# Ten of 22 gate and up column tiles of an encoder's feed-forward layers with seven block products in place of eight

## The chip, the cores and the metric

The kernel runs on one core of one Trainium2 chip. The metric is device time in microseconds (us) of one execution, as the median of the runs shown. Each change of layout of the inputs is made on the host before the launch and is not timed. Engines are named as the profile names them: PE is TensorE's matmuls and PEld its weight loads, DVE is VectorE, ACT is ScalarE, POOL is GpSimd, and SP is SyncE, which here only starts DMAs.

## The reference, cut to what is computed

Two layers over 512 tokens of 1024 features. Each layer is a half-step feed-forward block, a mixer with three attention branches, and a second feed-forward block, so there are four feed-forward blocks in all, each with 2816 hidden columns. The change is in these.

```
D_MODEL = 1024; SEQ = 512; DEPTH = 2; D_FF = 2816

def swiglu(h, w_gate, w_up, w_down):
    return (jax.nn.silu(h @ w_gate) * (h @ w_up)) @ w_down

for l in range(DEPTH):
    h = rms_norm(x, norm_g[l, 0])
    x = x + 0.5 * swiglu(h, ffn_w_gate[l, 0], ffn_w_up[l, 0], ffn_w_down[l, 0])
    ...                                    # mixer: x = x + merged @ w_o[l]
    h = rms_norm(x, norm_g[l, 2])
    x = x + 0.5 * swiglu(h, ffn_w_gate[l, 1], ffn_w_up[l, 1], ffn_w_down[l, 1])
return rms_norm(x, final_g)
```

## The kernel before, in words

Activations are held transposed: a tile has 128 features on the partitions and the 512 tokens along the free dimension, so `h` is eight such tiles (`KC` = 8). Each fp32 operand is split into a high part in the type fp32r and a low part, the fp32r of what is left (`hi` and `lo`). A product is then three matmuls for each tile of 128 features: high by high, high by low, low by high. `product` issues them as eight pairs (lines 96 and 97) and then eight more (line 99): 24 matmuls of 512 moving columns.

`ffn` walks over 22 column tiles of 128 hidden columns (`m`). For each it loads the gate's weights and the up weights, 512 KB each. `weights` starts the DMA on SP's queue into a `raw` tile (three buffers), ACT casts the high part (`whi`, line 82), and DVE subtracts to get the low part (`wlo`, line 83); `whi` and `wlo` have four buffers each. PE makes the two products into two PSUM tiles `mm` (three buffers). `gated` scales the gate by the norm's factor `rb` (line 295), ACT applies SiLU (line 296), DVE scales the up product (line 298), multiplies (line 299), and ACT and DVE split the result into `ghi` and `glo` (lines 106 and 108). After the 22 tiles the down product runs over eight output tiles of 66 matmuls each; `advance` adds each to the residual `x`, which lives in DRAM between uses (loaded and kept by DMAs on POOL's queue, `x_tile` and `x_keep`, two buffers of `x`), and makes the next block's `h` from it (`Norm.chunk`). The mixer ends in the same way over eight products with `w_o`. The last block ends in `finish` instead, which has the tokens on the partitions, and transposes `x` beforehand (`x_turned`).

The first block starts with `opening`, which works on the first two column tiles while its inputs are still arriving. The order of instructions on each engine is set when the program is built, by a scheduler with a cost model of its own; on the chip each engine's queue runs in that order, and an instruction that waits holds up all behind it on its engine. PE's sequence is the order of the code.

## Time and profile before

| what | us |
|---|---|
| median of 3 runs | 2484.22 (2482.74 to 2484.49) |
| the profiled execution's own time | 2485.75 |
| its span on the core | 2484.0 |
| PE busy | 2465.3 (99%), 11604 matmuls |
| DVE busy | 1294.3 (52%) |
| ACT busy | 1053.8 (42%) |

The span is what the profile divides up; the time of an execution has a little around it, here 1.75 us. Busy time of PE is modelled and overlapping, so what one matmul costs is read from the distance between starts, not from the durations. Rows of the timeline give the start, the duration, the engine, the line, the operation, and the tiles written and read.

### The profile page before, as it was taken

To read this page: it belongs to the slowest core of one execution; us is meant where nothing else is said; L and a number is where in the kernel's file an instruction comes from. 1 tells how busy PE (TensorE), PEld (TensorE's weight loads), DVE (VectorE), ACT (ScalarE), POOL (GpSimd) and SP (SyncE) were. 2 spreads that over 40 slices of the span, in tenths; PEclk is the share of its full clock that TensorE was granted. 3 is DMA by queue.
4 is the path that set the end of the run, shared out by engine and by line. 5 is a ranking of instruction groups with operands and counts; after the bars stand their busy time and mean duration, and the time that the engine had idled before them with its cause. 6 is when DMAs were issued, how large, how long until landed. Compare 5 with 4: busy or idle time off the path is not lost.

```text
span 2484.0 us, 30196 instructions
## 1 busy us (share of the span) xinstructions
PE 2465.3 (99%) x11604; PEld 2054.7 (83%) x11604; DVE 1294.3 (52%) x2178; ACT 1053.8 (42%) x1776; POOL 193.1 (8%) x300
## 2 busy tenths in 40 slices
PE   8999999999999999999999999999999999999998
PEld 7888888888888888888888888888888888888887
DVE  5444335766666644443344443367676766444432
ACT  5333225755557433332232332267555664333322
POOL 2000003311000000000000000033110001000000
PEclk9999999999999999999999999999999999999999
DMA  5323344432322342233432324443322224332232
GB/s 169 102 94 100 119 131 127 118 103 78 93 85 86 124 128 97 95 98 119 133 107 94 101 91 131 140 118 107 98 86 92 86 83 148 119 115 93 95 100 68
DMA packets 80655, 265.24 MB, mean 107 GB/s; under 512 B 10904, under 2 KB 16328, under 8 KB 80512
## 3 DMA queue, kind: packets, MB, share of 16 engines
q1 hardware_dynamic: 67680, 226.59, 29.4%
q0 software_dynamic: 11680, 34.86, 4.9%
q8 instruction: 92, 1.51, 0.2%
q10 hardware_dynamic: 1152, 1.86, 0.2%
q14 instruction: 51, 0.42, 0.1%
HBM read 241.22 MB, written 12.62 MB: 102 GB/s over the span
## 4 chain that ended last, share of the span: by engine, by line
PE 97%; DVE 1%; ACT 1%; issue 0%; DMA 0%; SPq 0%; POOLq 0%; POOL 0%; ACTq 0%; DVEq 0%
PE mm L96 22%; PE mm L97 22%; PE mm L99 22%; PE mm L288 5%; PE mm L290 5%; PE mm L287 5%; PE av L597 2%; PE t L587 1%; PE s L542 1%; PE s L543 1%; PE av L698 1%; PE mm L492 1%; PE mm L491 1%; PE mm L389 1%; PE mm L387 1%; PE mm L388 1%
## 5 line engine op out<-in xcount | busy, mean ns | idle before, releaser
L96 PE MATMUL mm<-h,whi 128*128 128x512 f32 x2112 | 831.7, 394 | 0.2
L97 PE MATMUL mm<-l,whi 128*128 128x512 f32 x2112 | 825.0, 391 | 0.0
L82 ACT CAST whi<-raw 128x1024 fp32r<-128x1024 f32 (+1 forms) x414 | 429.9, 1039 | 715.3 <-PE mm L97 372.7
L83 DVE TENSOR_TENSOR wlo<-raw,whi 128x1024 fp32r<-128x1024 f32 (+1 forms) x414 | 500.6, 1209 | 294.3 <-ACT whi L82 179.7
L99 PE MATMUL mm<-h,wlo 128*128 128x512 f32 x2112 | 521.8, 390 | 0.0
L99 PEld LDWEIGHTS mm<-h,wlo 128*128 128x128 f32 x2112 | 396.7, 188 | 82.2
L96 PEld LDWEIGHTS mm<-h,whi 128*128 128x128 f32 x2112 | 397.0, 188 | 80.7 <-issue 0.8
L97 PEld LDWEIGHTS mm<-l,whi 128*128 128x128 f32 x2112 | 397.3, 188 | 79.4
L298 DVE TENSOR_TENSOR un<-mm,rb 128x512 f32<-128x512 f32 x87 | 60.1, 691 | 296.8 <-PE mm L99 296.8
L288 PE MATMUL mm<-g,whi 128*128 128x512 f32 x528 | 205.7, 390 | 0.0
L287 PE MATMUL mm<-g,whi 128*128 128x512 f32 x528 | 205.6, 389 | 0.0
L106 ACT CAST g<-un 128x512 fp32r<-128x512 f32 x88 | 54.5, 620 | 251.4 <-DVE un L299 251.4
L290 PE MATMUL mm<-g,wlo 128*128 128x512 f32 x528 | 131.4, 390 | 0.0
L295 DVE TENSOR_TENSOR gn<-mm,rb 128x512 f32<-128x512 f32 x88 | 60.8, 691 | 133.4 <-PE mm L99 133.4
L556 ACT ACTIVATE lg<-lg,negm 128x256 f32<-128x256 f32 (+1 forms) x192 | 114.0, 594 | 25.2 <-DVE negm L553 23.7
L61 POOL DMA_DIRECT2D d_x<-x x40 | 22.1, 553 | 1262.9 <-DVE x L246 1262.6
L288 PEld LDWEIGHTS mm<-g,whi 128*128 128x128 f32 x528 | 99.2, 188 | 20.5
L290 PEld LDWEIGHTS mm<-g,wlo 128*128 128x128 f32 x528 | 99.2, 188 | 20.5
L287 PEld LDWEIGHTS mm<-g,whi 128*128 128x128 f32 x528 | 99.1, 188 | 20.5
L296 ACT ACTIVATE gn<-gn 128x512 f32<-128x512 f32 x88 | 55.8, 634 | 123.6 <-DVE gn L295 123.6
L108 DVE TENSOR_TENSOR g<-un,g 128x512 fp32r<-128x512 f32 x88 | 60.9, 692 | 62.8 <-ACT g L106 62.8
L246 DVE SCALAR_TENSOR_TENSOR x<-mm,x 128x512 f32<-128x512 f32 x40 | 27.7, 692 | 109.1 <-PE mm L290 72.4
(223 smaller groups left out, 3037.8 us busy)
## 6 DMA issues: line engine op xcount, KB each, us to landing
raw<-in_w_gu SPq DMA_DIRECT2D x172, 512.0 KB, 3.4
raw<-in_w_down SPq DMA_DIRECT2D x48, 512.0 KB, 3.5
raw<-in_w_gate SPq DMA_DIRECT2D x48, 512.0 KB, 3.5
raw<-in_w_qk SPq DMA_DIRECT2D x44, 512.0 KB, 3.6
raw<-in_w_branch SPq DMA_DIRECT2D x24, 512.0 KB, 3.5
raw<-in_w_last SPq DMA_DIRECT2D x22, 512.0 KB, 3.5
d_x<-x POOLq DMA_DIRECT2D x40, 256.0 KB, 2.4
x<-d_x POOLq DMA_DIRECT2D x40, 256.0 KB, 2.9
```

Of the source, the lines that this page charges most:

```text
L82: nc.scalar.copy(hi[:, w], raw[:, w])
L83: nc.vector.tensor_tensor(out=lo[:, w], in0=raw[:, w], in1=f(hi[:, w]), op=ALU.subtract)
L96: nc.tensor.matmul(ps, wh, xhi[k], start=k == 0, stop=False)
L97: nc.tensor.matmul(ps, wh, xlo[k], start=False, stop=False)
L99: nc.tensor.matmul(ps, wl, xhi[k], start=False, stop=k == n - 1)
L108: nc.vector.tensor_tensor(out=lo, in0=src, in1=f(hi), op=ALU.subtract)
L287: nc.tensor.matmul(ps, w[k][0], ghi[c + k], start=c + k == 0, stop=False)
L288: nc.tensor.matmul(ps, w[k][0], glo[c + k], start=False, stop=False)
L290: nc.tensor.matmul(ps, w[k][1], ghi[c + k], start=False, stop=c + k == MF - 1)
L295: nc.vector.tensor_tensor(out=gn, in0=pg, in1=h.rb, op=ALU.mult)
L298: nc.vector.tensor_tensor(out=un, in0=pu, in1=h.rb, op=ALU.mult)
L556: nc.scalar.activation(p, p, AF.Exp, bias=negm, scale=-1.0, accum_out=total)
```

## The change

In ten of the 22 column tiles (`SEVEN`; nine in the first block) the work of gate and up is arranged as a product of two matrices of 2 by 2 blocks. The rows of the first are gate and up, its columns the even and the odd tiles of features; the second has the even and the odd tiles of features as rows and the two halves of the tokens (256 each, `H`) as columns. Strassen's scheme in Winograd's form takes seven block products for this where the plain way takes eight. A block product covers four feature tiles and 256 tokens, so it is 12 matmuls of 256 moving columns, and a column tile takes 84 of these in place of 48 of 512.

The scheme needs sums of blocks. Those of the activations (`Sides`, four objects for each block, from the residual `x` times the norm's gain) are made once for each block and held in 16 tiles `side`. Those of the weights (S1 to S4, tiles `wsum`) are made for each of the ten tiles on DVE, and the three weight tiles that come of it are split as before (`parted`), with the eighth block (`w22`) split apart. The scheme's sums of products are made as far as possible in PSUM by accumulating, the rest by ACT copies and DVE additions. The diff, cut:

```diff
+SEVEN = (3, 4, 6, 7, 9, 10, 12, 13, 15, 16)
-    def advance(m, ps, nxt):
+    def advance(m, ps, rb, fp, nxt):
         t = x_tile(m)
-        nc.vector.scalar_tensor_tensor(out=t, in0=ps, scalar=0.5, in1=t, op0=ALU.mult, op1=ALU.add)
+        d = quarters(fp)[:, 0:2, :].rearrange("p a c -> p (a c)")
+        nc.vector.scalar_tensor_tensor(out=d, in0=ps, scalar=0.5, in1=rb, op0=ALU.mult, op1=ALU.mult)
+        nc.vector.tensor_tensor(out=t, in0=d, in1=t, op=ALU.add)
...
     def gated(h, fp, pg, pu, ghi, glo):
...
-        nc.vector.tensor_tensor(out=un, in0=pu, in1=h.rb, op=ALU.mult)
-        nc.vector.tensor_tensor(out=un, in0=un, in1=gn, op=ALU.mult)
+        nc.vector.tensor_tensor(out=un, in0=pu, in1=gn, op=ALU.mult)
...
+    class Sides:
+        def __init__(self, fp, h, p, xs):
...
+                    x = x_tile(k)
+                nc.scalar.activation(x, x, AF.Copy, scale=h.gain[:, k : k + 1])
...
+            nc.vector.tensor_tensor(out=t1, in0=b12, in1=b11, op=ALU.subtract)
+            nc.vector.tensor_tensor(out=t2, in0=b22, in1=t1, op=ALU.subtract)
+            nc.vector.tensor_tensor(out=t3, in0=b22, in1=b12, op=ALU.subtract)
+            nc.vector.tensor_tensor(out=t4, in0=b21, in1=t2, op=ALU.subtract)
+            both = [split(raw[:, n : n + 2, :].rearrange("p a c -> p (a c)"), fp, "side", 16) for n in (0, 2)]
...
+    def seven(l, i, m, h, fp, sides, ghi, glo):
...
+        ra, a11, a12 = raw(0)
+        wa = parted(ra)
+        rb, a21, a22 = raw(1)
+        w22 = [fp.tile([P, 4, P], F32R, tag=g, name=g) for g in ("w22h", "w22l")]
+        nc.scalar.copy(w22[0], a22)
+        nc.vector.tensor_tensor(out=w22[1], in0=a22, in1=f(w22[0]), op=ALU.subtract)
...
+        nc.vector.tensor_tensor(out=s1, in0=a21, in1=a22, op=ALU.add)
+        nc.vector.tensor_tensor(out=s3, in0=a11, in1=a21, op=ALU.subtract)
+        w13 = parted(r1)
+        nc.vector.tensor_tensor(out=s2, in0=s1, in1=a11, op=ALU.subtract)
+        nc.vector.tensor_tensor(out=s4, in0=a12, in1=s2, op=ALU.subtract)
+        w24 = parted(r2)
...
+        block_product(pa[:, 0], blocks(wa, 0, 2 * P), [s.b11 for s in sides], start=True)
+        block_product(pr[:, 0], blocks(w13, 0), side(1), start=True)
+        nc.scalar.copy(u2, pa[:, 0])
+        block_product(pv[:, 0], [[t[:, k, :] for k in range(4)] for t in w22], side(4), start=True, stop=True)
+        nc.scalar.copy(pv[:, 1], pr[:, 0])
+        block_product(pa[:, 0], blocks(wa, P, 2 * P), [s.b21 for s in sides])
+        block_product(pa[:, 1], blocks(w24, 0), side(2), stop=True)
+        nc.vector.tensor_tensor(out=u2, in0=pa[:, 1], in1=u2, op=ALU.add)
+        nc.scalar.copy(c11, pa[:, 0])
+        block_product(pr[:, 0], blocks(w24, S), [s.b22 for s in sides])
+        block_product(pr[:, 1], blocks(w13, S), side(3), stop=True)
+        nc.vector.tensor_tensor(out=gu[:, 1:3], in0=pr, in1=u2.unsqueeze(1).to_broadcast([P, 2, H]), op=ALU.add)
+        nc.vector.tensor_tensor(out=c21, in0=pv, in1=u3.unsqueeze(1).to_broadcast([P, 2, H]), op=ALU.add)
+        nc.vector.tensor_tensor(out=gn, in0=gn, in1=h.rb, op=ALU.mult)
+        nc.scalar.activation(gn, gn, AF.Silu)
         nc.vector.tensor_tensor(out=un, in0=un, in1=gn, op=ALU.mult)
+        keep(fp, un, ghi, glo)
```

The fourth block product accumulates onto the first one's result, so PE waits before it until ACT has copied that result to `u2`. In every ordinary tile one DVE multiplication by `rb` goes; `advance` has one more DVE instruction in its place, and `finish` takes the factor from a small tile. `Sides` is emitted after the second tile (after the third in the first block, where it reads the inputs already on chip). In `finish`'s block the transposes of `x` move from tiles 4 to 11 to tiles 17 to 20, two in each, with four small ACT copies for each in place of one. Tiles `g` of the late columns, `x` of the opening and other small buffers share space with the new tiles. The three buffers of `raw`, four of `whi` and `wlo`, two of `x` and three of `mm` stay as they were.

How the queues change is shown at three places. The numbers in the names tell one use of a tile from another; what stands in brackets is what the instruction waits for (DMAHW and DMASW are landings of DMAs).

On DVE, in the middle of the first block, one ordinary column tile before:

```order
L295 TENSOR_TENSOR gn_1063<-mm_1013,rb_357 128x512 [waits PE_49]
L83 TENSOR_TENSOR wlo_1147<-raw_1145,whi_1146 128x1024 [waits DMAHW3_49,Activation_49]
L298 TENSOR_TENSOR un_1066<-mm_1038,rb_357 128x512 [waits PE_49]
L83 TENSOR_TENSOR wlo_1153<-raw_1151,whi_1152 128x1024 [waits DMAHW4_49,Activation_49]
L299 TENSOR_TENSOR un_1066<-un_1066,gn_1063 128x512 [waits DVE_49]
L108 TENSOR_TENSOR g_1071<-un_1066,g_1069 128x512 [waits Activation_49]
```

On DVE now, while PE is in ordinary tile 11 (`gu_1458` is its work): the end of tile 10 (`gu_1298`), the sums for tile 12 (`raw_1466`, `wsum_1485`) and those for tile 13 (`raw_1593`, `raw_1599`, `wsum_1605`, `wsum_1612`):

```order
L389 TENSOR_TENSOR wsum_1485<-wsum_1478,raw_1466 128x512
L390 TENSOR_TENSOR wsum_1485<-raw_1466,wsum_1485 128x512 [waits DVE_49]
L431 TENSOR_TENSOR gu_1298<-gu_1298 128x512 [waits Activation_49]
L385 TENSOR_TENSOR wsum_1605<-raw_1599 128x512 [waits DMAHW6_49]
L332 TENSOR_TENSOR gu_1458<-mm_1408,rb_357 128x512 [waits PE_49]
L120 TENSOR_TENSOR g_1394<-gu_1298,g_1392 128x512 [waits Activation_49]
L95 TENSOR_TENSOR wlo_1489<-wsum_1485,whi_1488 128x1024
L386 TENSOR_TENSOR wsum_1605<-raw_1593,raw_1599 128x512 [waits DMAHW5_49]
L389 TENSOR_TENSOR wsum_1612<-wsum_1605,raw_1593 128x512 [waits DVE_49]
L390 TENSOR_TENSOR wsum_1612<-raw_1593,wsum_1612 128x512 [waits DVE_49]
L334 TENSOR_TENSOR gu_1458<-mm_1433,gu_1458 128x512 [waits PE_49,Activation_49]
L95 TENSOR_TENSOR wlo_1596<-raw_1593,whi_1595 128x1024 [waits Activation_49]
```

A landing of a DMA now stands between DVE's sums: `raw_1599` is the third `raw` buffer over again, the one that held `raw_1466`, whose last reader is the L390 two rows above it.

On ACT at that place before, one tile:

```order
L82 CAST whi_1080<-raw_1079 128x1024 [waits DMAHW2_49,PE_49,Activation_49]
L106 CAST g_997<-un_994 128x512 [waits DVE_49]
L82 CAST whi_1146<-raw_1145 128x1024 [waits DMAHW3_49,PE_49,Activation_49]
L296 ACTIVATE gn_1063<-gn_1063 128x512 [waits DVE_49,Activation_49]
L82 CAST whi_1152<-raw_1151 128x1024 [waits DMAHW4_49,PE_49,Activation_49]
```

and now, from the cast of S2 and S4 for tile 12 to the copy of tile 12's first block product (`u2`, L415):

```order
L94 CAST whi_1488<-wsum_1485 128x1024 [waits DVE_49,PE_49]
L118 CAST g_1392<-gu_1298 128x512 [waits DVE_49]
L333 ACTIVATE gu_1458<-gu_1458 128x512 [waits DVE_49]
L86 CAST whi_1595<-raw_1593 128x1024 [waits DMAHW5_49,PE_49]
L118 CAST g_1462<-gu_1458 128x512 [waits DVE_49]
L415 COPY gu_1495<-mm_1492 128x256 [waits PE_49,Activation_49]
```

The copy for which PE waits stands behind the cast of tile 11's result (`g_1462`), which waits for DVE's L334 above.

At the end of a down product, DVE before (`x_2628` is the last of the eight residual tiles, `l7_2635` its low part for the next product):

```order
L83 TENSOR_TENSOR wlo_2758<-raw_2756,whi_2757 128x1024 [waits DMAHW1_49,PE_49,Activation_49]
L246 SCALAR_TENSOR_TENSOR x_2628<-mm_2561,x_2628 128x512 [waits DMASW7_49,DMASW0_49,PE_49]
L83 TENSOR_TENSOR wlo_2788<-raw_2786,whi_2787 128x1024 [waits DMAHW2_49,Activation_49]
L127 SCALAR_TENSOR_TENSOR l7_2635<-x_2628,ng_75,h7_2633 128x512 [waits Activation_49]
L137 TENSOR_TENSOR acc_1959<-acc_1959,sq_2637 128x512 [waits Activation_49]
```

and now:

```order
L259 SCALAR_TENSOR_TENSOR gu_3173<-mm_3104,rb_357 128x512 [waits PE_49]
L87 TENSOR_TENSOR wlo_3333<-raw_3331,whi_3332 128x1024 [waits DMAHW2_49,Activation_49]
L260 TENSOR_TENSOR x_3171<-gu_3173,x_3171 128x512 [waits DMASW7_49,DMASW0_49,DVE_49]
L139 SCALAR_TENSOR_TENSOR l7_3180<-x_3171,ng_75,h7_3178 128x512 [waits Activation_49]
L149 TENSOR_TENSOR acc_2490<-acc_2490,sq_3182 128x512 [waits Activation_49]
```

The residual is now made in two instructions with a weight's low part between them.

At the end of the mixer, ACT before (`h7` is the last tile of the next block's input):

```order
L125 ACTIVATE h6_7548<-x_7543,ng_75 128x512 [waits DVE_49]
L136 ACTIVATE sq_7552<-x_7543 128x512 [waits Activation_49]
L82 CAST whi_7697<-raw_7696 128x1024 [waits DMAHW0_49,PE_49]
L125 ACTIVATE h7_7591<-x_7586,ng_75 128x512 [waits DVE_49]
L136 ACTIVATE sq_7595<-x_7586 128x512 [waits Activation_49]
```

and now:

```order
L137 ACTIVATE h6_8093<-x_8088,ng_75 128x512 [waits DVE_49]
L148 ACTIVATE sq_8097<-x_8088 128x512 [waits Activation_49]
L86 CAST whi_8240<-raw_8239 128x1024 [waits DMAHW0_49,PE_49]
L348 ACTIVATE x_8303<-x_8303,ng_75 128x512 [waits DMASW5_49,DMASW1_49,DMASW6_49,DVE_49,Activation_49]
L137 ACTIVATE h7_8136<-x_8131,ng_75 128x512 [waits DVE_49]
L148 ACTIVATE sq_8140<-x_8131 128x512
```

The first `x` of `Sides` has come in ahead of `h7`, and waits for its DMA.

More of the change, by code (lines that the diff above doesn't have):

```diff
@@ L83, in weights, with parted @@
             nc.vector.tensor_tensor(out=lo[:, w], in0=raw[:, w], in1=f(hi[:, w]), op=ALU.subtract)
+        return hi, lo
+    def parted(src, dst=None):
+        hi = wpool.tile([P, 1024], F32R, tag="whi", name="whi")
+        lo = wpool.tile([P, 1024], F32R, tag="wlo", name="wlo")
+        nc.scalar.copy(hi, src)
+        nc.vector.tensor_tensor(out=lo, in0=src, in1=f(hi), op=ALU.subtract)
         return hi, lo
@@ L253, in ffn @@
             first = l == 0 and i == 0
+            xs = [None] * KC
             xt = None
             if first:
-                opening(l, i, h, fp, ghi, glo)
+                xs = opening(l, i, h, fp, ghi, glo)
+            sides = []
             for m in range(2 if first else 0, MF):
+                if m in (SEVEN[1:] if first else SEVEN):
+                    if not sides:
+                        sides = [Sides(fp, h, p, xs) for p in range(4)]
+                    seven(l, i, m, h, fp, sides, ghi, glo)
+                    continue
                 wg = weights(a["w_gu"][l, i, m, 0])
@@ L267, in ffn @@
                     h.finish()
-                if m == 4 and first:
+                if m == 5 and first:
                     position_tables()
                     small_values()
-                if nxt is None and 4 <= m < 4 + KC:
-                    if m == 4:
-                        xt = fp.tile([P, 4, D], F32, tag="xt", name="xt")
-                    x_turned(xt, m - 4)
+                if nxt is None and MF - 5 <= m < MF - 1:
+                    if xt is None:
+                        xt = x_room(fp)
+                    for k in range(2):
+                        x_turned(xt, 2 * (m - MF + 5) + k)
                 gated(h, fp, pg, pu, ghi, glo)
+                if m == (2 if first else 1):
+                    sides = [Sides(fp, h, p, xs) for p in range(4)]
             if nxt is None:
-                finish(fp, ghi, glo, xt)
+                finish(fp, ghi, glo, xt, h)
                 return
@@ L290, in ffn, with quarters, keep @@
                         nc.tensor.matmul(ps, w[k][1], ghi[c + k], start=False, stop=c + k == MF - 1)
-                advance(m, ps, nxt)
+                advance(m, ps, h.rb, fp, nxt)
+    def quarters(fp):
+        return fp.tile([P, 5, H], F32, tag="gu", name="gu", bufs=2)
+    def keep(fp, un, ghi, glo):
+        late = len(ghi) > SEVEN[-1]
+        hi, lo = split(un, fp, "side" if late else "g", 16 if late else GBUFS)
+        ghi.append(hi)
+        glo.append(lo)
     def gated(h, fp, pg, pu, ghi, glo):
-        gn = fp.tile([P, S], F32, tag="gn", name="gn", bufs=2)
+        t = quarters(fp).rearrange("p a c -> p (a c)")
+        gn, un = t[:, 0:S], t[:, S : 2 * S]
@@ L299, in gated @@
         nc.vector.tensor_tensor(out=un, in0=un, in1=gn, op=ALU.mult)
-        hi, lo = split(un, fp, "g", 2 * MF)
-        ghi.append(hi)
-        glo.append(lo)
+        keep(fp, un, ghi, glo)
     def opening(l, i, h, fp, ghi, glo):
@@ L312, in opening @@
         raws = [wpool.tile([P, 1024], F32, tag="raw", name="raw", bufs=3) for _ in range(3)]
-        raws.append(fp.tile([P, 1024], F32, tag="raw4", name="raw4"))
+        raws.append(fp.tile([P, 1024], F32, tag="sum", name="raw4", bufs=2))
         def load(k, queue):
-            xs[k] = fp.tile([P, S], F32, tag=f"xf{k}", name="xf")
+            xs[k] = fp.tile([P, S], F32, tag="g", name="xf", bufs=GBUFS)
             queue.dma_start(xs[k], a["xT"][k])
@@ L358, in opening, with x_room @@
         gated(h, fp, ps[2], ps[3], ghi, glo)
+        return xs
+    def x_room(fp):
+        side = [fp.tile([P, S], F32, tag="side", name="xt", bufs=16) for _ in range(6)]
+        t = fp.tile([P, 2, S], F32, tag="sum", name="xt", bufs=2)
+        side += [t[:, 0], t[:, 1]]
+        return [side[2 * t : 2 * t + 2] for t in range(4)]
     def x_turned(xt, k):
@@ L365, in x_turned, with finish @@
             nc.tensor.transpose(pt[:, j, :], t[:, j * P : (j + 1) * P], ident)
-        nc.scalar.copy(xt[:, :, k * P : (k + 1) * P], pt)
-    def finish(fp, ghi, glo, xt):
+        for j in range(4):
+            nc.scalar.copy(xt[j][k // 4][:, k % 4 * P : (k % 4 + 1) * P], pt[:, j])
+    def finish(fp, ghi, glo, xt, h):
         half = D // 2
-        fg = fp.tile([P, D], F32, tag="fg", name="fg")
+        fg = fp.tile([P, D], F32, tag="sum", name="fg", bufs=2)
         nc.scalar.dma_start(fg, a["final_g"].to_broadcast([P, D]))
@@ L421, in finish @@
             nc.gpsimd.tensor_tensor(out=r, in0=r, in1=nhalf[:, 0:1], op=ALU.pow)
[L422 removed]
+            x0 = xt[t][0]
             nc.scalar.activation(x0, x0, AF.Copy, scale=r)
```

55 lines of the change are left out of this document (50 added, 5 removed).

## The prediction

> **What bounds the kernel now.** I read first the page: the busy row of the engines, the clock by slices, and the chain that ended last.
>
> ```profile
> PE 2465.3 (99%) x11604; PEld 2054.7 (83%) x11604; DVE 1294.3 (52%) x2178; ACT 1053.8 (42%) x1776; POOL 193.1 (8%) x300
> PEclk9999999999999999999999999999999999999999
> PE 97%; DVE 1%; ACT 1%; issue 0%; DMA 0%; SPq 0%; POOLq 0%; POOL 0%; ACTq 0%; DVEq 0%
> ```
>
> PE is the bound from end to end at a full clock, so PE time saved counts, as long as DVE (52%) and ACT (42%) still deliver in time. Then I read PE's timeline, in an ordinary column tile and where the mixer has matmuls of 256 columns.
>
> ```profile
> 150.73 0.39 PE L96 MATMUL mm<-h,whi 128*128 128x512 f32 x1
> 154.36 1.98 PE L99 MATMUL mm<-h,wlo 128*128 128x512 f32 x8
> 156.17 0.39 PE L96 MATMUL mm<-h,whi 128*128 128x512 f32 x1
> 161.61 0.39 PE L96 MATMUL mm<-h,whi 128*128 128x512 f32 x1
> ...
> 493.82 0.28 PE L491 MATMUL mm<-whi,h 128*128 128x256 f32 x1
> 495.74 1.13 PE L494 MATMUL mm<-wlo,h 128*128 128x256 f32 x8
> 496.71 0.28 PE L542 MATMUL s<-qk 128*128 128x256 f32 x1
> ```
>
> A tile of 48 matmuls takes 161.61 - 150.73 = 10.88 us, 226.7 ns each. Sixteen matmuls of 256 columns, each with new weights, take 495.74 - 493.82 = 1.92 us, 120.0 ns each. Half the columns cost 53%.
>
> **PE's gain.** A changed tile is 84 x 0.120 = 10.08 us, 0.80 less. In 9 + 3 x 10 = 39 tiles that is 31.2 us (1.26%). The transposes only move, at the same count.
>
> Here a rule can be weighed. The Trainium skill's TensorE: Matmul & The Clock Gate (Back-to-back issue gap) gives 518 cycles for 512 columns and 262 for 256 at 2.4 GHz, 215.8 and 109.2 ns; by it, as an estimate, a tile would gain 1.19 us and the sum 46 us. The rows above disagree by about 11 ns on either, and the measurement decides.
>
> **DVE and ACT in the changed tiles.** These rows price their work and the handing over between engines.
>
> ```profile
> 150.93 0.69 DVE L295 TENSOR_TENSOR gn<-mm,rb 128x512 f32<-128x512 f32 x1 [1.64 <-PE mm L99]
> 156.37 0.69 DVE L298 TENSOR_TENSOR un<-mm,rb 128x512 f32<-128x512 f32 x1 [3.62 <-PE mm L99]
> 156.98 1.22 DVE L83 TENSOR_TENSOR wlo<-raw,whi 128x1024 fp32r<-128x1024 f32 x1
> 158.11 0.69 DVE L299 TENSOR_TENSOR un<-un,gn 128x512 f32<-128x512 f32 x1
> 159.48 0.69 DVE L108 TENSOR_TENSOR g<-un,g 128x512 fp32r<-128x512 f32 x1 [0.69 <-ACT g L106]
> ...
> 151.72 0.63 ACT L296 ACTIVATE gn<-gn 128x512 f32<-128x512 f32 x1 [1.50 <-DVE gn L295]
> 154.60 1.05 ACT L82 CAST whi<-raw 128x1024 fp32r<-128x1024 f32 x1 [2.25 <-PE mm L97]
> 158.83 0.62 ACT L106 CAST g<-un 128x512 fp32r<-128x512 f32 x1 [3.18 <-DVE un L299]
> ...
> L590 DVE TENSOR_TENSOR pl<-t,ph 128x256 fp32r<-128x256 f32 x64 | 26.8, 419 | 3.3 <-ACT ph L589 2.9
> L589 ACT CAST ph<-t 128x256 fp32r<-128x256 f32 x64 | 23.5, 367 | 25.2 <-PE t L587 24.7
> L125 ACT ACTIVATE h<-x,ng 128x512 fp32r<-128x512 f32 x40 | 29.0, 724 | 47.2 <-DVE x L246 47.2
> ...
> raw<-in_w_gu SPq DMA_DIRECT2D x172, 512.0 KB, 3.4
> x<-d_x POOLq DMA_DIRECT2D x40, 256.0 KB, 2.9
> ```
>
> From start to start DVE takes 0.61 us for 512 elements (156.37 to 156.98) and 1.13 for 1024 (156.98 to 158.11); a dependent one follows at its full 0.69; 256 take about 0.34 (0.42 less the same overlap). DVE to ACT is 0.10 (150.93 + 0.69 to 151.72), ACT to DVE 0.03 (158.83 + 0.62 to 159.48), ACT after PE's last use of a buffer 0.24 (154.36 to 154.60).
>
> A changed tile needs on DVE three splits of 1024, ten instructions of 512 (w22, S1 to S4, two sums of products, `rb`, the product, `glo`) and one of 256: 3 x 1.13 + 10 x 0.61 + 0.34 = 9.8 us of PE's 10.08; an ordinary one 2 x 1.13 + 3 x 0.61 = 4.1. Two changed and one ordinary are 23.7 us of DVE in 31.04 of PE (10.08 x 2 + 10.88). The total fits; what decides is the order. I follow one round by hand, pair 9 and 10, ordinary 11, then 12, with zero at tile 9's start on PE and 1.44 us for a block product.
>
> - At 9.60 PE has read the high part of tile 9's seventh product's weights; ACT may cast S2, S4 of tile 10 into that buffer: 9.84 to 10.89.
> - DVE from 10.92: that low part 1.13, tile 9's sum 0.61, a low part of 11 at 1.13, the second sum 0.61, `rb` 0.69: 15.09.
> - SiLU (0.10 + 0.63 + 0.03), product 0.69, cast (0.10 + 0.62 + 0.03): 17.29. DVE had nothing else there.
> - DVE then, in its order: `glo` 9, S1 of 12, low part of 11, `u2` of 10, `w22` of 12, S3 of 12, low part, sum of 10, low part, second sum, `rb`, S2, S4: eight of 0.61, three of 1.13, one of 0.34 and S4 at a full 0.69 with 0.08 for its dependence, 9.4: 26.7. The SiLU and casts for these run beside.
> - Only now is the `raw` buffer of tile 12's first weights free for tile 13's second, and S1 of 13 stands next but one on DVE. The DMA takes 3.4 and 0.08 at its ends: 30.15. DVE stands still for some 3 us.
> - DVE: S1 of 13, `gn` 11, `glo` 10, low part of 12, S3, S2, S4 (0.08 more), product of 11: 5.5, 35.7.
> - ACT casts tile 11's result (0.10 + 0.62), then copies tile 12's `u2` (0.37, 0.10 of it overlapped); with 0.07 to PE the fourth block product may start at 36.8.
>
> PE wants it at 31.04 + 3 x 1.44 = 35.36. So PE waits 1.4 us, and with a slow first matmul after it 1.5, in each round; the next round starts later by as much, so it is not made up. A round costs 32.5 us against 32.64 before: the gain of two tiles, 1.6, is nearly all given back. This wait comes at tiles 6, 9, 12 and 15 of three blocks and at 9, 12, 15 of the first (there tile 4 stands alone, and the same sum leaves tile 6 half a us to spare): 15 x 1.5 = 22.5 us.
>
> **The first pair in blocks two to four.** `Sides` goes through two `x` buffers in four rounds: each is a load (0.4 to issue, 2.9), two ACT scales at 0.63 and four DVE instructions of 0.34, 6 us at least, with waits for casts and ordinary work in the same queues. The second `x` comes when the last residual is stored.
>
> ```profile
> 881.25 0.55 POOL L56 DMA_DIRECT2D x<-d_x  x1 [2.62 <-DMA d_x<-x]
> 886.53 0.55 POOL L56 DMA_DIRECT2D x<-d_x  x1 [2.46 <-DMA d_x<-x]
> 882.23 0.39 PE L96 MATMUL mm<-h,whi 128*128 128x512 f32 x1
> 883.15 0.72 ACT L125 ACTIVATE h<-x,ng 128x512 fp32r<-128x512 f32 x1 [1.48 <-DVE x L246]
> 885.63 0.39 PE L97 MATMUL mm<-l,whi 128*128 128x512 f32 x1
> ...
> 373.97 0.69 DVE L246 SCALAR_TENSOR_TENSOR x<-mm,x 128x512 f32<-128x512 f32 x1 [2.80 <-PE mm L290]
> 374.58 1.22 DVE L83 TENSOR_TENSOR wlo<-raw,whi 128x1024 fp32r<-128x1024 f32 x1
> 375.71 0.75 DVE L127 SCALAR_TENSOR_TENSOR l<-x,ng,h 128x512 fp32r<-128x512 f32 x1
> 377.17 0.39 PE L97 MATMUL mm<-l,whi 128*128 128x512 f32 x1
> ...
> 33.45 0.69 DVE L295 TENSOR_TENSOR gn<-mm,rb 128x512 f32<-128x512 f32 x1
> 34.38 0.39 PE L96 MATMUL mm<-h,whi 128*128 128x512 f32 x1
> ```
>
> From 4.3 us into the block (886.53 - 882.23) four such rounds of 6 to 6.5 end at 28 to 30, and what stands behind on DVE (three `side` and `gn` instructions, a low part, S2, S4: 4.4) puts tile 3's S4 near 33.9. Then the same DMA wait (3.5), three sums and a low part of DVE, a cast and the copy (4.1): 41.5. Tile 3 starts near 34.8 and wants its fourth product at 39.1: 2.4 us. Nothing and 4 us bound it; three blocks, 7 us.
>
> **At the seams.** After a down product the residual's second instruction comes behind the low part, at 375.71; then `h7` to 377.22 and `l7` to 378.0, with 0.07 to PE, which wants it at 377.17: 0.9 us, three times. After the mixer the first `x` lands at 881.25 + 2.9 = 884.15, its scale precedes `h7` (before at 883.15) and moves it to 884.83 to 885.55, `l7` to 886.3 against 885.63: 0.8, twice. Together 4.3; bounds 0 (if the scheduled waits fall elsewhere) and 7. In the opening the sums of `Sides` (about six DVE instructions before `gn`, now at 33.45) move `gn` past 34.38, when PE wants the bank: 1.0, between 0 and 3. SP has no more DMAs, POOL eight more loads in each of three blocks, of which only those above are waited for. The late transposes' `x` loads (2.9) have a tile of 10.88 us to land, and the small ACT copies lie beside PE. The instruction saved in ordinary tiles is off the path: nothing.
>
> **The sum.** -31.2 + 22.5 + 7 + 4.3 + 1.0 = +3.6 us on the profiled execution (span 2484.0, time 2485.75, 1.5 above the median). On the median of 2484.2 that is 2488. A measurement tells about 0.2%, 5 us, from no change.
>
> **Rivals.**
> 1. DVE is early enough, so the landing is hidden: no waits in the pairs, and 2484.2 - 31.2 + 5.3 = 2458. For it: 7 us of DVE are free in a round. Against it: buffer and order tie S1 to S4 by the DMA, and DVE would have to be 1.4 us earlier. 17%.
> 2. Half of that: a round is 1 us shorter, from overlaps that I take too small. 2484.2 - 31.2 + 15 x 0.5 + 3 x 1.3 + 5.3 = 2470. 12%.
> 3. DVE's new shapes (sums over strided blocks, a broadcast operand) run longer than the 0.69 of plain ones. Ten of them stand in a round's chain, so 0.1 us on each is 1 us, 15 us in all: 2503. It decides for slower from 0.01 us on each (1.5 us above the forecast). No row shows such a shape slower, or at all. 13%.
> 4. The matmuls of a changed tile don't keep 120 ns; 1 ns is 3.3 us. The 256-column rows are the same operation, with weights new in each, so I fold this into the range.
>
> The forecast has 58%, with a range of its own of 2480 to 2496; it splits into faster 6, same 28, slower 24. With the rivals: faster 0.35, same 0.28, slower 0.37. The range over all reaches into the first and third: 2460 to 2503.
>
> **What would show it.** After: 13008 matmuls, 256-column ones 0.120 apart. In tiles 9 to 11 PE's waits at the fourth block product, about 1.5 us, released by ACT's `u2` copy; DVE idle near 3 us before S1 of each pair's second tile, released by a landing; a round of 32.5 us. I am wrong if these waits are absent (rival 1), or if the round is over 33 with DVE instructions longer than 0.7.

## The result, and the profile after

The changed kernel takes 2461.78 us (median of 4 runs, 2460.08 to 2466.55) against 2483.94 before: the ratio is 0.9916, with an interval of 0.9903 to 0.9928. That is 22 us faster, where the prediction had 2488 and gave faster a chance of 0.35. The time is within 4 us of the first rival's, 2458. A second set of runs of the same kernel gave 2461.56 (2458.19 to 2468.34).

The page of the changed kernel, its busy row, the clock by slices, and the chain by engine:

```profile
PE 2437.5 (99%) x13008; PEld 2094.9 (85%) x13008; DVE 1517.9 (62%) x2562; ACT 1184.3 (48%) x2057; POOL 207.7 (8%) x324
PEclk9999999999999999999999999999999999999999
PE 95%; DVE 1%; issue 1%; DMA 1%; ACT 1%; POOL 0%; POOLq 0%; ACTq 0%; DVEq 0%
```

PE is still the bound. The span went from 2484.0 to 2459.3 us, 24.7 less, and all of it lies on PE's own line: from its first matmul to its last are 2470.9 us before and 2446.1 after. So 6.5 of the 31.2 us were given back, not 34.8 as forecast.

The round that the prediction worked out by hand (pair 9 and 10, tile 11, then 12 and 13) starts here at 110.17. PE's timeline of tile 12, its first, fourth and next tile's first block product:

```profile
141.23 0.28 PE L400 MATMUL mm<-h,whi 128*128 128x256 f32 x1
...
145.54 0.28 PE L400 MATMUL mm<-h,whi 128*128 128x256 f32 x1
...
151.30 0.28 PE L400 MATMUL mm<-h,whi 128*128 128x256 f32 x1
```

The tile takes 151.30 - 141.23 = 10.07 us, 119.9 ns for each of 84 matmuls. The round takes 141.23 - 110.17 = 31.06, where 31.04 was the ideal and 32.5 the forecast. The fourth block product comes 4.31 us after the first, without a wait. DVE's timeline around the landing for which it was to stand still:

```profile
129.24 0.69 DVE L386 TENSOR_TENSOR wsum<-raw 128x512 f32<-128x512 f32 x1
...
133.91 0.68 DVE L389 TENSOR_TENSOR wsum<-wsum,raw 128x512 f32<-128x512 f32 x1
134.63 0.69 DVE L390 TENSOR_TENSOR wsum<-raw,wsum 128x512 f32<-128x512 f32 x1
135.24 0.69 DVE L431 TENSOR_TENSOR gu<-gu 128x512 f32<-128x512 f32 x1
135.84 0.68 DVE L385 TENSOR_TENSOR wsum<-raw 128x512 f32<-128x512 f32 x1
...
141.50 0.69 DVE L334 TENSOR_TENSOR gu<-mm,gu 128x512 f32<-128x512 f32 x1 [0.70 <-PE mm L111]
```

L386 is S3 of tile 12, L390 its S4, L385 S1 of tile 13. S1 follows with no idle time. At the end DVE waits 0.70 us for PE's tile 11, not the other way round. SP's queue in the same stretch shows why:

```profile
129.99 0.33 SPq L370 DMA_DIRECT2D raw<-in_w_gu  x1
135.39 0.33 SPq L85 DMA_DIRECT2D raw<-in_w_gu  x1
```

And ACT's timeline shows how much time is left before PE needs the copy:

```profile
142.22 0.62 ACT L118 CAST g<-gu 128x512 fp32r<-128x512 f32 x1 [1.55 <-DVE gu L334]
142.92 0.38 ACT L415 COPY gu<-mm 128x256 f32<-128x256 f32 x1
```

The load for tile 13's second weights is issued at 129.99, right behind the end of S3 (129.93), and not behind S4 (135.32). S3 is the last reader of the *second* weights of tile 12. The addresses in the built program agree: the tile `raw_1599` lies at 71584 like `raw_1472`, the second weights of tile 12; `raw_1466`, the first, lies at 75680 and goes to tile 14. The `u2` copy ends at 143.30, 2.24 us before PE wants its fourth product.

By stretch, from the starts of the down products on PE (254.09, 1123.02 and 1483.49 before, 246.87, 1109.76 and 1462.64 after; each down stage takes 119.68 in both): counted from PE's first matmul, the first block gained 7.3 us of its 7.2 (9 tiles by 0.80), the first mixer with block 2 gained 6.0 of 8.0, block 3 7.6 of 8.0, and all that follows 3.9 of 8.0. Most of what was given back is at the ends of the mixers, 1.2 and 4.0 us. The second mixer's end on ACT:

```profile
2094.78 0.72 ACT L348 ACTIVATE x<-x,ng 128x512 f32<-128x512 f32 x1 [4.19 <-DMA x<-d_x]
2095.40 0.71 ACT L137 ACTIVATE h<-x,ng 128x512 fp32r<-128x512 f32 x1
```

On PE:

```profile
2096.16 0.49 PE L108 MATMUL mm<-h,whi 128*128 128x512 f32 x1 [1.68 <-ACT h L137]
2096.95 0.79 PE L109 MATMUL mm<-l,whi 128*128 128x512 f32 x1 [0.29 <-DVE l L139]
2097.54 3.21 PE L111 MATMUL mm<-h,wlo 128*128 128x512 f32 x8
```

And a window over these slow matmuls (length, then busy time and instructions of PE, PEld, DVE, ACT and POOL, the granted clock, and DMA):

```profile
2098.00:2100.20 2.20, 2.20 (x7) 1.71 (x6) 0.00 (x0) 0.82 (x1) 0.07 (x1) 0.52 0.45 119
```

`Sides`' scale of x (L348) stands ahead of `h7` (L137) on ACT and waits for its load, as the prediction said. PE loses 2.4 us by waiting, measured by the starts. Then come some eight matmuls at a granted clock of 0.52 and 427 ns, 1.6 us more. The first mixer's end costs 1.2 us at 879.33 and 880.12. In the profiles of other kernels below, the two places cost 1 to 11 us together, by run.

In the opening, DVE's timeline:

```profile
29.08 0.42 DVE L354 TENSOR_TENSOR tsum<-xf,tsum 128x256 f32<-128x256 f32 x1
29.41 0.42 DVE L355 TENSOR_TENSOR tsum<-xf 128x256 f32<-128x256 f32 x1
29.75 0.15 DVE L169 TENSOR_SCALAR rt<-st 128x4 f32<-128x4 f32 x1
29.82 1.22 DVE L87 TENSOR_TENSOR wlo<-raw,whi 128x1024 fp32r<-128x1024 f32 x1
30.95 0.42 DVE L356 TENSOR_TENSOR tsum<-xf,tsum 128x256 f32<-128x256 f32 x1
31.29 0.68 DVE L120 TENSOR_TENSOR side<-tsum,side 128x512 fp32r<-128x512 f32 x1
```

POOL's, after:

```profile
29.99 1.95 POOL L170 TENSOR_TENSOR rs<-rt,nhalf 128x4 f32<-128x4 f32 x1 [11.01 <-DVE rt L169]
```

POOL's, before:

```profile
30.94 1.04 POOL L158 TENSOR_TENSOR rs<-rt,nhalf 128x4 f32<-128x4 f32 x1 [11.82 <-DVE rt L157]
```

PE's, after:

```profile
32.00 0.65 PE L176 MATMUL st<-ident,rs 128*128 128x128 f32 x4 [2.19 <-POOL rs L170]
```

`rt`, from which POOL takes the power for the norm's factor, stands behind two sums of `Sides` on DVE. The power then takes 1.95 us in place of 1.04, beside a DVE subtraction that ends at 31.04; in the kernel before, no DVE instruction ran beside it. PE's start at 32.00 is 2.35 us later than its pace without a wait would give. In this one profile the first inputs came sooner than in that of before (waits of 1.0 at 6.77 and 0.4 us at 8.88 against 3.4 at 9.10), 2.0 us in sum, so the first block as a whole kept its full gain by luck. Why they came sooner, no run here settles.

### The profile page after: what moved, and what is told of

It reads as the page before. It is cut to its first block, busy times and chain, and to the rows that moved or that the text cites. A ratio compares the mean times of both kernels' runs of the same rounds, so it can differ in the third digit from the quotient of the medians.

```text
span 2459.3 us, 33723 instructions
## 1 busy us (share of the span) xinstructions
PE 2437.5 (99%) x13008; PEld 2094.9 (85%) x13008; DVE 1517.9 (62%) x2562; ACT 1184.3 (48%) x2057; POOL 207.7 (8%) x324
## 3 DMA queue, kind: packets, MB, share of 16 engines
q8 instruction: 102, 1.67, 0.3%
## 4 chain that ended last, share of the span: by engine, by line
PE 95%; DVE 1%; issue 1%; DMA 1%; ACT 1%; POOL 0%; POOLq 0%; ACTq 0%; DVEq 0%
PE mm L111 16%; PE mm L108 16%; PE mm L109 16%; PE mm L313 5%; PE mm L312 5%; PE mm L315 5%; PE mm L400 2%; PE pr L403 2%; PE pr L401 2%; PE pr L400 2%; PE mm L403 2%; PE mm L401 2%; PE av L738 2%; PE t L728 1%; PE s L683 1%
## 5 line engine op out<-in xcount | busy, mean ns | idle before, releaser
L86 ACT CAST whi<-raw 128x1024 fp32r<-128x1024 f32 (+1 forms) x336 | 347.7, 1036 | 509.1 <-PE mm L109 196.2
L108 PE MATMUL mm<-h,whi 128*128 128x512 f32 x1488 | 587.7, 395 | 2.4 <-ACT h L137 2.2
L109 PE MATMUL mm<-l,whi 128*128 128x512 f32 x1488 | 582.2, 391 | 0.6 <-DVE l L139 0.6
L87 DVE TENSOR_TENSOR wlo<-raw,whi 128x1024 fp32r<-128x1024 f32 (+1 forms) x336 | 405.5, 1207 | 256.6 <-ACT whi L86 145.8
L111 PE MATMUL mm<-h,wlo 128*128 128x512 f32 x1488 | 368.9, 390 | 0.0
L111 PEld LDWEIGHTS mm<-h,wlo 128*128 128x128 f32 x1488 | 280.3, 188 | 58.5
L108 PEld LDWEIGHTS mm<-h,whi 128*128 128x128 f32 x1488 | 279.7, 188 | 59.0 <-ACT h L137 3.9
L109 PEld LDWEIGHTS mm<-l,whi 128*128 128x128 f32 x1488 | 279.9, 188 | 56.7 <-DVE l L139 2.0
L312 PE MATMUL mm<-g,whi 128*128 128x512 f32 x408 | 158.7, 389 | 0.0
L313 PE MATMUL mm<-g,whi 128*128 128x512 f32 x408 | 158.7, 389 | 0.0
L95 DVE TENSOR_TENSOR wlo<-wsum,whi 128x1024 fp32r<-128x1024 f32 x78 | 95.2, 1220 | 44.5 <-ACT whi L94 44.5
L334 DVE TENSOR_TENSOR gu<-mm,gu 128x512 f32<-128x512 f32 x48 | 33.1, 689 | 86.1 <-PE mm L111 86.1
```

Source lines behind the costliest of these rows:

```text
L86: nc.scalar.copy(hi[:, w], raw[:, w])
L87: nc.vector.tensor_tensor(out=lo[:, w], in0=raw[:, w], in1=f(hi[:, w]), op=ALU.subtract)
L108: nc.tensor.matmul(ps, wh, xhi[k], start=k == 0, stop=False)
L109: nc.tensor.matmul(ps, wh, xlo[k], start=False, stop=False)
L111: nc.tensor.matmul(ps, wl, xhi[k], start=False, stop=k == n - 1)
L312: nc.tensor.matmul(ps, w[k][0], ghi[c + k], start=c + k == 0, stop=False)
```

## The experiments

The theory after the result (A): buffers are given out as they fall free and not in turn, so no landing stands in DVE's way, and DVE has room. The rival (B): buffers don't matter and DVE was only overpriced. Ratios are against the kernel before, with their intervals.

**The three `raw` buffers strictly in turn.**

```diff
+    def raw_tile():
+        n = turn_raw[0] % 3
+        turn_raw[0] += 1
+        return wpool.tile([P, 1024], F32, tag=f"raw{n}", name="raw", bufs=1)
```

> The three raw buffers are three tiles used strictly in turn. Theory A (what my forecast got wrong is the rule by which buffers are given out: not in turn but in the order in which they come free): with them in turn the second load of a pair's second tile must follow S4 of the first tile, 5 us later than in the changed kernel (there it was issued at 129.99, S3 ended at 129.93, S4 at 135.33). The scheduler has put three DVE instructions more ahead of S1 of the second tile, which take up 1.8 us of it, so DVE should stand 0.5 to 1 us for the landing. PE's fourth block product waited for nothing and had 2.2 us to spare after the u2 copy (112.23 against 114.49), so the time stays at 2462, at most 2466. The forecast's own chain would still give 1.5 us in each of 15 rounds: 2484. Theory B (buffers don't matter, DVE was simply overpriced): load issued right after S3 or DVE without any wait for a landing, 2462.

Measured: 2463.68 us (2458.22 to 2472.22), 0.9921 [0.9906, 0.9936]. SP at the same place:

```profile
134.69 0.33 SPq L377 DMA_DIRECT2D raw<-in_w_gu  x1
```

DVE there:

```profile
133.94 0.69 DVE L397 TENSOR_TENSOR wsum<-raw,wsum 128x512 f32<-128x512 f32 x1
...
137.04 0.68 DVE L127 TENSOR_TENSOR g<-gu,g 128x512 fp32r<-128x512 f32 x1
138.10 0.69 DVE L392 TENSOR_TENSOR wsum<-raw 128x512 f32<-128x512 f32 x1 [0.38 <-DMA raw<-in_w_gu]
```

The load now follows S4 (ended 134.63), and DVE stands for the landing, but 0.38 us and not 3: the scheduler, which knows of the buffer, has put other work first (tile 10's product, tile 11's gate, the low part of S2 and S4, and tile 10's `glo`). PE does not wait. So the mechanism exists, and buffers do matter to the loads. The forecast had joined a real order of instructions to an assumed use of buffers, and these two belong to different programs.

**`whi` and `wlo` in turn as well.**

```diff
+        return wpool.tile([P, 1024], F32R, tag=f"{g}{n}", name=g, bufs=1)
```

> As the one before, and the four whi and wlo buffers are used strictly in turn too. Theory A: the cast of S2 and S4 of a pair's second tile then starts when PE has read the seventh product's high part, at 9.84 us of the tile before as I had worked out by hand, not at 8.42 as in the changed kernel. With 1.4 us later here and 0.5 to 1 us of DVE standing for the landing, the 2.2 us to spare are used up to 0 or a little below: rounds of 31.1 to 31.6 us, 2462 to 2470. My forecast's full chain: rounds of 32.5, 2484. Theory B: no change at all, 2462, and rounds of 31.06.

Measured: 2463.29 us (2461.58 to 2469.74), 0.9922 [0.9910, 0.9933]; pairs start every 31.06 us, and the `u2` copy keeps its 2.25 us before nearly every fourth product. All the buffers that the forecast assumed in turn are in turn here, and the wait is not there. The cast of S2 and S4 of tile 10 did begin 9.80 us into the round, as the forecast's 9.84 had it, but the scheduler had moved the sums of tile 12 forward, and its S4 ended at 19.9 in place of the forecast's 26.7. So the expected loss of slack did not come either. In time and pace (B) foretold this run better than (A); what speaks against (B) is the run before it, where the load moved behind S4 with its buffer. Both have it that DVE has room, and that is what keeps the time. No run joins the forecast's order of instructions to buffers in turn, so the forecast's wait in the rounds was never produced.

**How late may DVE be?** S2 is computed three times in each changed tile (the diff), or five times.

```diff
-        nc.vector.tensor_tensor(out=s2, in0=s1, in1=a11, op=ALU.subtract)
+        for _ in range(3):
+            nc.vector.tensor_tensor(out=s2, in0=s1, in1=a11, op=ALU.subtract)
```

> In each changed tile S2 is computed three times in place of once: two more DVE instructions of 512 (1.2 us by their distance) in the chain of sums, 2.4 us in a round of two changed tiles and an ordinary one, in which DVE is busy 73.59 of 93.20 us, so 6.5 of 31.06 free. Theory (order and buffers leave DVE room, PE's fourth product has 2.25 us to spare): no wait, 2460 to 2466. The forecast's chain, in which DVE's time in a round counts in full: 13 rounds or so and six pairs by 2.4 us, 2490 to 2500.

> S2 computed five times: four more, 2.4 us in each changed tile, 4.9 in a round of 6.5 free. Theory: two changed tiles beside each other then need 2 x (9.8 + 2.4) = 24.4 us of DVE in 20.2 of PE, made up in the ordinary tile; the low parts of S2 and S4 come late by up to 2 us, and PE begins to wait, 0 to 2 us a round: 2462 to 2490. Forecast's chain: 2520 and more.

Measured: 2459.53 us (2458.96 to 2462.16), 0.9906 [0.9892, 0.9919], and 2465.82 (2463.40 to 2469.67), 0.9931 [0.9918, 0.9945]. Windows over three rounds of the first block (the columns as above), of the changed kernel:

```profile
78.00:172.00 94.00, 94.00 (x650) 87.50 (x649) 74.79 (x111) 47.83 (x70) 3.21 (x6) 1.00 0.32 107
```

With two more:

```profile
78.00:172.00 94.00, 94.00 (x652) 87.83 (x651) 81.25 (x122) 47.93 (x70) 3.22 (x6) 1.00 0.32 107
```

With four more:

```profile
78.00:172.00 94.00, 94.00 (x650) 87.28 (x649) 88.90 (x134) 45.48 (x69) 3.22 (x6) 1.00 0.32 104
```

DVE goes from 74.79 to 81.25 and 88.90 us of 94, and PE loses nothing in this stretch. In the third kernel the copy's lead before the fourth product falls to 0.05 to 2.25 us, and PE begins to wait here and there (0.9 us at 1271), 2.3 us in all by the starts of the tiles. So 2.4 us more of DVE in a round are free. Twice that is 4 us slower in the median, which the overlapping intervals do not set apart from nothing; the profile shows 2.3 of it as waits. The forecast's chain had charged every such microsecond to PE.

**More tiles with seven products.** Tiles 3, 4 and 6 to 16; then all of 3 to 16.

```diff
+SEVEN = (3, 4, 6, 7, 8, 9, 10, 11, 12, 13, 14, 15, 16)
```

> Seven products in tiles 3, 4 and all of 6 to 16 of each block (without 3 in the first): three tiles more in each of four blocks, 12 x 0.80 = 9.6 us less of PE. A changed tile needs 9.8 us of DVE by my count of 0.61 and 1.13 us starts, PE 10.08. Theory A (buffers come as they fall free, DVE's queue keeps ahead): PE doesn't wait in the run of eleven, tiles 10.08 apart: 2452. Theory of the forecast (DVE's queue meets landings and is late): with no ordinary tile to recover in, DVE falls behind by 0.5 to 1.5 us in each tile of the run, tiles 10.6 to 11.6 apart, 44 tiles: 2475 to 2520.

Measured: 2451.48 us (2450.62 to 2453.16), 0.9872 [0.9859, 0.9885]: the fastest of all, 10 us below the changed kernel for 12 tiles more. A window in the run of eleven:

```profile
101.00:181.00 80.00, 80.00 (x669) 80.00 (x668) 77.49 (x111) 44.47 (x72) 0.00 (x0) 1.00 0.31 100
```

DVE is busy 97% and PE doesn't wait; tiles start 10.08 apart. A changed tile's 9.8 us of DVE, as the prediction counted them, fit into 10.08. Outside that window PE waits once for `u2`, 1.4 us in the first pair of block 3.

> Seven products in all of tiles 3 to 16 (in the first block without 3 and 5): 12 + 3 x 14 = 54 tiles in place of 39 (51 in the run with 13). Theory: DVE keeps up with 9.8 us in 10.08 (it did in the run of eleven, busy 97%), so 3 x 0.80 = 2.4 less than 2451.5: 2449. Rival: the first pair has no ordinary tile behind it in which DVE makes up for Sides, and PE waits 1 to 5 us in tiles 4 to 8 of three blocks: 2452 to 2464.

Measured: 2456.02 us (2454.56 to 2456.70), 0.9889 [0.9875, 0.9902]: more tiles and 4.5 us slower. A window in the third block:

```profile
1299.00:1400.00 101.00, 98.33 (x814) 97.66 (x813) 94.79 (x135) 55.59 (x89) 0.00 (x0) 1.00 0.34 105
```

One of PE's waits in it:

```profile
1310.86 0.39 PE L400 MATMUL pr<-h,whi 128*128 128x256 f32 x1 [0.77 <-ACT pv L417]
```

In blocks 3 and 4 PE waits about 1.1 us in every third tile, for ACT's copy of `pv`, and loses 3.8 us in the first tiles of block 3; in block 2 it does not wait. The rival's cost is there in number, but its waits in the first tiles came in one block of three, and those in every third tile neither expectation had. Between these two kernels lies the point from which the order on DVE and ACT decides: 13 tiles with an ordinary one behind the first pair are inside it, 14 in a row outside.

> As the one before, and POOL multiplies x by the gain for Sides in place of ACT. Theory: the waits of PE at the ends of the two mixers (0.6 to 7.5 us, by run) go, since h7 on ACT no longer has the scale ahead of it: 3 us less than the one before. Rival: DVE's first sum still waits ahead of l7, now for a slower POOL, whose queue also issues the loads of x: the same waits or up to 3 us more each, and the first pair waits for Sides.

```diff
-                nc.scalar.activation(x, x, AF.Copy, scale=h.gain[:, k : k + 1])
+                nc.gpsimd.tensor_scalar(x, x, h.gain[:, k : k + 1], None, op0=ALU.mult)
```

Measured: 2488.27 us (2487.52 to 2492.51), 1.0022 [1.0014, 1.0031]. PE's waits at the mixers' ends for `h7` are gone, but POOL takes 1.73 us for each scale there, and 2.0 in the opening, where eight of them stand ahead of the power and PE waits 6.3 us. At the mixers' ends, too, the power now stands behind a scale on POOL, and PE waits 2.8 us (at 894.42) and 2.4 us (at 2125.88) for it. The first tiles of blocks 2 to 4 lose 7.8, 8.8 and 8.8 us in place of 0, 3.8 and 0. Both the theory's part and the rival's came, and the rival's is larger.

**The scale of x behind `h7`.** The gain for `Sides` is made from `l7` in blocks 2 to 4, or from `rb` in the first block only, through a small new tile.

```diff
+        g = small.tile([P, 8], F32, tag="lg8", name="lg8", bufs=1)
+        nc.vector.scalar_tensor_tensor(out=g[:, 0:KC], in0=after, scalar=0.0, in1=h.gain[:, 0:KC], op0=ALU.mult, op1=ALU.add)
```

> The gain by which Sides scales x is taken from a small tile that is made from l7, so in blocks 2 to 4 the scale can't stand ahead of h7 on ACT. Theory: the two waits of PE where a mixer ends (1.2 us at 879 and 2.4 us with 1.6 us of half clock behind it at 2096, 5.2 us together) go: 2461.8 - 5 = 2457. Rival 1: Sides comes later by 1 to 2 us, and the first pair waits for it instead: 2461. Rival 2: h7 comes late for another reason (the residual's own load on POOL): no change, 2462.

> Only in the first block the gain for Sides is made from rb, so Sides starts after 33 us in place of 25. Theory: PE's wait of 2.35 us at 32.0 (the transposes of rs, released by POOL's pow, which came late since rt stood behind Sides' sums on DVE, and took 1.95 us in place of 1.04) falls to less than 0.3: 2459.5. Rival: Sides, 8 us later, isn't ready when tile 4 starts at 56.1, and PE waits there: 2462 or more.

Measured: 2472.42 us (2472.34 to 2481.23), 0.9966 [0.9954, 0.9978], and 2477.76 (2473.00 to 2482.18), 0.9980 [0.9971, 0.9989]. The waits that were to go did go in both, yet both are slower than the changed kernel, by 11 and 16 us, and in no way that was expected. The cause is in neither wait. In both traces the 512-column matmuls that stream `g`, `side`, `yp` or `mh` stand 231 to 235 ns apart in place of 227, and those that stream `h` do not. The new tile had moved these tiles by 32 bytes. Six kernels were run to find out whether the address does it:

> The changed kernel and one small tile of 8 columns (32 bytes) more, set once at the start and read by nothing, which moves the tiles of the pools behind it (ffn with g, side; mix with yp, mh) by 32 bytes and leaves h and l where they are. In the two kernels that came out slow (the gain from l7: 2472; the gain from rb: 2478), which have such a tile too, the 512-column matmuls that stream g, side, yp or mh stood 233 to 235 ns apart in place of 227 (some 3900 of them), those that stream h 227. Theory: it is the address; here too those stand 233 to 235 apart, and the 256-column ones that stream side 116 to 118; 3900 x 6.4 ns = 25, less 2 to 7 of the rest: 2478, from 2472 to 2487. Rival: it came from the order of instructions or from that chip's mood: 227 everywhere and 2462.

Measured: 2465.21 us (2458.14 to 2471.42), 0.9925 [0.9908, 0.9942]. Matmuls at 227: the pad fell into a gap and moved nothing, so this run says nothing on the address.

> The changed kernel, its instructions and their order untouched, with 32 bytes set aside ahead of the pools ffn and mix, so that g, side, yp and mh start at 64 modulo 128 in place of 32; h, l, whi and wlo stay at 32. (In the kernel with the pad of 8 columns that came before, the pad fitted into a gap, and these tiles stood where they were, at 32: the addresses of the built program say so, and its matmuls were 227 apart.) Theory address: the 512-column matmuls that stream g, side, yp and mh 233 to 235 apart, some 3900, 25 us; the 256-column ones with side 118; time 2475 to 2482. Rival order: 227 and 2462.

```diff
+    shim = ctx.enter_context(tc.tile_pool(name="shim", bufs=1))
+    pad = shim.tile([P, 8], F32, tag="pad", name="pad")
```

Measured: 2482.52 us (2475.29 to 2484.55), 0.9988 [0.9979, 0.9997]. The same order of instructions, and nearly the whole gain is lost. PE in the first block's down products, here:

```profile
301.45 2.03 PE L318 MATMUL mm<-g,wlo 128*128 128x512 f32 x8
303.32 0.39 PE L315 MATMUL mm<-g,whi 128*128 128x512 f32 x1
```

In the changed kernel:

```profile
300.82 1.98 PE L315 MATMUL mm<-g,wlo 128*128 128x512 f32 x8
302.63 0.39 PE L312 MATMUL mm<-g,whi 128*128 128x512 f32 x1
```

Eight matmuls take 1.87 us, 233.8 ns each, against 1.81, 226.3. Matched one by one with those of the changed kernel, the 512-column matmuls take 20.1 us more in sum, and the 256-column ones 2.5 us less. The profiled executions are 21.8 us apart, and the rest is mostly a wait of 6.1 us at the first mixer's end in this run, where the changed kernel had 0.6.

> As the one before with 96 bytes: g, side, yp and mh at 0 modulo 128, the weights still at 32. If what counts is the address of the streamed operand alone, 0 is a fourth value beside 32 (227), 64 (233 to 235) and 96 (229 to 232), and I can't tell which side it falls; by the trend it is 225 to 230, and the time 2455 to 2475. If it is the distance to the weights' address (0 at 227, 32 at 234, 64 at 229 to 232), 96 may be slow again, 230 to 235, 2470 to 2482.

Measured: 2476.41 us (2475.33 to 2491.01), 0.9985 [0.9973, 0.9998]; matmuls of `g` 230 to 238 apart. At 0 modulo 128, with the weights left at 32, it is slow too.

> A constant tile is 24 columns (96 bytes) wider, and every tile behind it moves by 96 bytes: h, l, weights, g, side, yp, mh all at 0 modulo 128. If the address of the streamed operand alone counts, h too takes the value that g has in the run with 96 bytes, in all 13008 matmuls. If the distance between streamed operand and weights counts, it stays at 227 and 120, and the time at 2462.

Measured: 2457.45 us (2457.30 to 2457.68), 0.9897 [0.9883, 0.9910]; 227 and 120 everywhere. A streamed operand at 0 is slow with the weights at 32 and fast with the weights at 0, and weights at 32 are fast or slow by the operand. So what counts is the distance between the streamed operand and the weights modulo 128, not either address alone; distances other than 0 were run with the weights at 32 only. That this kernel's median is 4 us below the changed kernel's is not explained. The run beside these, of the changed kernel itself:

> The changed kernel once more, beside these: 2460 to 2466, the 512-column matmuls 227 apart; the wait at the opening and the two at the ends of the mixers (2.4, 1.2 and 2.4 with 1.6 at half clock in the first profile) within 2 us of these.

Measured: 2461.56 us (2458.19 to 2468.34), 0.9919 [0.9904, 0.9933]; waits of 1.7 at the opening, and 0.8 and 1.9 at the mixers' ends, so these differ from run to run by up to 2 us each.

With the small tile 64 bytes wide, which puts the distance at 64 (matmuls of `g` 229 apart in the median), the two kernels came out so:

> The gain of Sides made from l7 in blocks 2 to 4, as before, with the small tile 16 columns (64 bytes) wide. Theory (address, and the scale of x ahead of h7): matmuls at 227 again, and PE's waits at 879 and 2096 (1.2, and 2.4 with 1.6 at half clock) gone: 2461.8 - 5 = 2457. Rival 1: the address has nothing to do with it and the order itself costs: 2472 again. Rival 2: the seam's waits come back at the first pair: 2462.

Measured: 2463.12 us (2462.30 to 2471.83), 0.9928 [0.9916, 0.9940]. DVE at the first mixer's end:

```profile
878.60 0.69 DVE L1063 SCALAR_TENSOR_TENSOR x<-mm,x 128x512 f32<-128x512 f32 x1 [1.82 <-DMA x<-d_x]
```

PE in the first pair of block 2:

```profile
921.17 0.39 PE L411 MATMUL mm<-h,whi 128*128 128x256 f32 x1 [2.60 <-ACT gu L426]
```

At the second mixer's end the wait is gone. At the first the residual itself comes late, since its x is still being loaded, and PE waits 1.5 us. In block 2 it waits 1.9 us for DVE's L334 at 897.66, and its first pair now waits 2.8 us at its fourth product for the `u2` copy: the wait that the forecast had for the first pairs, with `Sides` late. The waits were moved rather than removed: both rivals, in part.

> The gain of Sides in the first block made from rb, the small tile 64 bytes wide. Theory: PE's wait of 2.35 us at 32.0 falls below 0.3 (it did in the 32-byte form) and no matmul is slower: 2461.8 - 2.2 = 2459.6. Rival: address irrelevant: 2477 again.

Measured: 2464.63 us (2463.50 to 2466.76), 0.9925 [0.9912, 0.9937]. The power takes 1.04 us from 28.49, the transposes follow at 29.61 in place of 32.00, and PE doesn't wait. The cause of the opening's wait is shown; the gain of 2 us is eaten by the distance of 64 (some 6 us net, by the matmuls' starts in the run before).

## Why the prediction was wrong

- **PE's gain** (31.2 us): right. 84 matmuls take 10.07 us, 13008 matmuls, no loss of pace; rival 4 was nothing.
- **DVE's durations** (rival 3): right to discard. The broadcast sums take 0.68 us, the strided ones 0.68 to 0.69. The total of 9.8 us for a tile held too, as the run of eleven tiles showed.
- **The round by hand** is where it failed: its wait of 1.5 us, 22.5 us in the sum, is not there in any round (all take 31.06). Two bullets were wrong. "At 9.60 PE has read the high part ... ACT may cast S2, S4 of tile 10 into that buffer: 9.84": the cast began at 118.58, 8.41 us into the round (row below), since it got the buffer of tile 9's S2 and S4 (both at 47008), which PE reads last in the sixth product, 1.44 us before the seventh; from there everything came 1.4 to 1.6 us sooner than by hand (S4 of tile 12 ended at 25.15, not 26.7). "Only now is the `raw` buffer of tile 12's first weights free for tile 13's second": it was the second weights' buffer, free 5.4 us earlier, at S3. That alone took out the "some 3 us" that DVE was to stand still, and S1 of tile 13 began at 25.67 in place of 30.15. The `u2` copy ended at 33.13 in place of 36.7. PE wanted it at 35.37, as the prediction had it (35.36).
- The sentence ahead of the prediction, that `raw_1599` is the buffer that held `raw_1466`, is wrong in the same way: the order of rows doesn't tell which buffer a name stands for. The 22.5 us (15 x 1.5) rest on these two steps. That either alone would have left PE without a wait is worked out, not run: S1 at 30.15 less the 1.5 us makes the copy end near 35.2, and PE wants it at 35.36.

```profile
118.58 1.05 ACT L94 CAST whi<-wsum 128x1024 fp32r<-128x1024 f32 x1
```

- **The first pairs** (7 us): the same landing was added, and it wasn't there. The copy ended 0.1 to 1 us before PE's fourth product in tile 3 of the three blocks: near, but no wait (0.04 us in one).
- **The seams** (4.3) and **the opening** (1.0), together 5.3 against 6.5 measured, are near in sum by luck: the parts are off both ways, and the 6.5 has in it the 2.0 us by which the first inputs came sooner. The three down products' seams, 0.9 each, cost some 0.25. The residual came late as forecast (`l7`, the first row below, ended at 370.72). But "PE's sequence is the order of the code", ahead of the prediction, doesn't hold here: in the built program three matmuls of the up product (with `h0`, `l0` and `h1`) stand ahead of the gate's last one, with `l7`, which starts at 370.79. Before the change the order at this place was that of the code.

```profile
369.97 0.75 DVE L139 SCALAR_TENSOR_TENSOR l<-x,ng,h 128x512 fp32r<-128x512 f32 x1 [0.79 <-ACT h L137]
...
369.72 0.76 PE L108 MATMUL mm<-h,whi 128*128 128x512 f32 x2
370.32 0.39 PE L109 MATMUL mm<-l,whi 128*128 128x512 f32 x1
370.55 0.40 PE L108 MATMUL mm<-h,whi 128*128 128x512 f32 x1
370.79 0.49 PE L109 MATMUL mm<-l,whi 128*128 128x512 f32 x1
```

The mixers' ends, 0.8 each by the mechanism as described, cost 1.2 and 4.0: the load of x came later than counted, and behind the longer wait PE ran at half clock. In the opening the forecast had PE waiting for `gn` to free a PSUM bank; it waited for POOL's power, 2.35 us in place of 1.0. The sums of `Sides` were the cause in both, the path was another.
- **The chances.** Rival 1 was argued down with "buffer and order tie S1 to S4 by the DMA", which was an inference and not a row. It had the outcome, no waits in the pairs, and its condition that DVE be 1.4 us earlier came true (1.4 to 1.6); that the load itself left 5.4 us sooner it didn't have. Its number, 2458, is within 4 us, with the luck at the seams in it.

## What to carry to other kernels

In a pool whose buffers are given out by a scheduler, which buffer a tile gets is part of the schedule: look for the reader whose end comes just ahead of the load's issue in a trace, or for the addresses, before building a wait upon it. A chain worked out by hand, in which each link is a little late, needs its slack written beside each link; here, by the working above, a wait needed two late links at once, and they had to use up the 2.2 us by which the copy came ahead of PE's need. And a small tile more in a pool can move all that lies behind it: compare the pace of matmuls that should be alike before explaining a loss by waits.
